# Down products of a feed-forward layer in a seven-product form, with two of four weight sums made by adding loads

## The chip, the cores and the metric

One core of a Trainium2 chip runs the whole program. The metric is the device time of one execution in microseconds, the median over runs; lower is better. The matmul engine is called PE, the vector engine DVE, the scalar engine ACT, GpSimd POOL; SP only issues DMAs.

## What is computed

One inference step of a two-layer encoder trunk for 512 prompt and 64 sample tokens, 576 columns in all, in fp32. A layer is a half-step feed-forward, three attention mixers with one output projection, a cross-attention over memory, and a second half-step feed-forward. Only the feed-forward is touched:

```
def half_ffn(x, g, w_gate, w_up, w_down):
    h = rms_norm(x, g)
    return 0.5 * ((jax.nn.silu(h @ w_gate) * (h @ w_up)) @ w_down)
```

D_MODEL is 1024 (8 row tiles of 128), D_FF is 2816 (22 tiles). There are four such blocks: two layers, two half-steps each. The sum is added to x.

## The kernel before

**Layout and precision.** Activations are transposed: a tile has 128 features as partitions and 576 tokens as columns, worked in two halves of 288 columns (`HALVES`, or L and R in the helpers). Each fp32 operand is split into a high part (a cast by ACT, at times by DVE) and a low part (what the high part leaves, a subtraction on DVE), and each product is three matmuls: high x high, high x low, low x high. Weights arrive by DMA in `stage` buffers and are split into `whi` and `wlo` (`parts`, `take`); hidden tiles into `hhi` and `hlo`.

**A feed-forward block** (`ffn`). The first 4 gate and up tiles (`PLAIN`) are ordinary products (`gemm`, banks g and u). The other 18 come in pairs through `rows2`, a seven-product form of a 2x2 block product: rows are a pair of output tiles, columns are the two halves of the tokens, and inner tiles are paired even and odd. It takes four weight blocks a11, a12, a21, a22 of 512 columns and makes four sums of them on DVE or POOL (`c1` to `c4`, tiles named `wc`); the moving side uses sums made by `combine_x`. Seven products of 4 x 3 matmuls stand in for eight. They run in PSUM banks P (a running sum that ACT copies out between products, tiles `cw`) and Q. Then `gate` applies silu, multiplies gate by up and splits the hidden tile. The down projection takes the hidden tiles in four chunks (`FFN_CHUNKS`, 4 + 6 + 6 + 6 tiles): for every chunk and each of 8 row tiles an ordinary product in bank d, after which DVE adds half of it to x (`stt` in `ffn`). Down work of a chunk is spread among the gate and up work of the next (`ffn_steps`).

**Order.** The program is first recorded as operations with costs and priorities and then put in an order by `Program.order`, a list scheduler: weight work gets an earlier priority by `ahead`, some operations may go to DVE or POOL, buffers come from pools by tag (`slots`: 49 `s` of 576 columns, 11 `b`, 3 `stage`, 6 `hi`, 6 `lo`, 8 PSUM banks). Every engine's queue is in order. All loads and stores are issued by SP.

All instructions are issued from one helper line (`issue`), so profile rows are told apart by tile names.

## Time and profile before

| | us |
|---|---|
| median of 3 runs (2452.07 to 2453.89) | 2452.24 |
| the profiled execution | 2451.2 |
| its span, first to last instruction | 2449.4 |
| PE busy | 2426.8 |
| DVE busy | 1849.4 |
| ACT busy | 1395.1 |
| POOL busy | 179.9 |

The rows further down come from that one execution. Busy time is the union of an engine's instructions; a matmul's length is its time in the pipeline, so the distance between starts tells its cost. The four feed-forward blocks lie at about 0 to 407, 840 to 1232, 1232 to 1624 and 2057 to 2449 us.

### The profile page before, as it was taken

How to read it: one execution, taken by the hardware profiler on the slowest of the kernel's cores; microseconds unless marked ns; L12 is line 12 of the kernel's file. 1: busy time of each engine (PE TensorE's matmuls, PEld its weight loads, DVE VectorE, ACT ScalarE, POOL GpSimd, SP SyncE). 2: the span in 40 equal slices, each digit the busy share in tenths (PEclk: the TensorE clock that was granted, in tenths of full speed). 3: DMA queues.
4: the chain of work that ended last, by engine and by line, in shares of the span. 5: the costliest groups of instructions: out<-in, count | busy, mean ns of one | idle time of the engine just before them, and what ended most of it. 6: DMA issues, size and time to landing. Idle time of an engine off the chain costs nothing.

```text
span 2449.4 us, 46161 instructions
## 1 busy us (share of the span) xinstructions
PE 2426.8 (99%) x18150; PEld 2387.5 (97%) x18150; DVE 1849.4 (76%) x3726; ACT 1395.1 (57%) x2857; POOL 179.9 (7%) x186
## 2 busy tenths in 40 slices
PE   8999999999999999999999999999999999999999
PEld 8999999999999999999999999999999999999999
DVE  8776766789886887776687767676898869876663
ACT  6554445679765754444455544465897666454442
POOL 1000000002110110000020000000111001100000
PEclk9999999999999999999999999999999999999999
DMA  4222333222332122223223222331223421222322
GB/s 149 93 89 84 95 102 117 67 70 87 109 132 78 53 91 89 85 87 96 91 78 96 89 93 85 108 123 56 73 87 116 130 65 66 78 93 93 93 84 91
DMA packets 77449, 224.17 MB, mean 92 GB/s; under 512 B 8880, under 2 KB 13040, under 8 KB 77232
## 3 DMA queue, kind: packets, MB, share of 16 engines
q1 hardware_dynamic: 77232, 221.23, 28.2%
q8 instruction: 142, 2.33, 0.4%
q14 instruction: 75, 0.61, 0.1%
HBM read 208.33 MB, written 12.86 MB: 90 GB/s over the span
## 4 chain that ended last, share of the span: by engine, by line
PE 89%; DVE 8%; ACT 2%; issue 1%; DMA 0%; SPq 0%; DVEq 0%; ACTq 0%
PE d L401 23%; PE P L401 19%; PE Q L401 14%; PE pj L401 7%; PE wo L401 4%; PE g L401 3%; PE u L401 3%; PE mq L401 2%; PE mo L401 2%; PE cq L401 2%; PE st L401 1%; PE O L401 1%; PE S L401 1%; PE ckv L401 1%; DVE wlo L401 1%; PE mv L401 1%
## 5 line engine op out<-in xcount | busy, mean ns | idle before, releaser
L401 ACT ACTIVATE whi<-stage 128x512 fp32r<-128x512 f32 (+1 forms) x649 | 387.8, 599 | 506.4 <-PE P L401 175.6
L401 DVE TENSOR_TENSOR wlo<-stage,whi 128x512 fp32r<-128x512 f32 (+1 forms) x706 | 466.1, 667 | 227.2 <-ACT whi L401 216.4
L401 PE MATMUL d<-hhi,wlo 128*128 128x288 f32 x1408 | 415.1, 295 | 0.0
L401 PE MATMUL d<-hlo,whi 128*128 128x288 f32 x1408 | 414.8, 295 | 0.0
L401 PE MATMUL d<-hhi,whi 128*128 128x288 f32 x1408 | 414.3, 294 | 0.0
L401 ACT ACTIVATE whi<-wc 128x512 fp32r<-128x512 f32 x280 | 177.0, 633 | 283.4 <-PE d L401 152.4
L401 DVE TENSOR_TENSOR wlo<-wc,whi 128x512 fp32r<-128x512 f32 x288 | 198.8, 690 | 145.2 <-ACT whi L401 144.1
L401 PEld LDWEIGHTS d<-hlo,whi 128*128 128x128 f32 x1408 | 264.1, 188 | 0.0
L401 PEld LDWEIGHTS d<-hhi,whi 128*128 128x128 f32 x1408 | 264.1, 188 | 0.0
L401 PEld LDWEIGHTS d<-hhi,wlo 128*128 128x128 f32 x1408 | 264.1, 188 | 0.0
L401 PE MATMUL pj<-xhi,whi 128*128 128x288 f32 x576 | 171.5, 298 | 0.0
L401 PE MATMUL P<-xbl,whi 128*128 128x288 f32 x576 | 169.8, 295 | 0.7 <-DVE xbl L401 0.7
L401 PE MATMUL P<-xbh,wlo 128*128 128x288 f32 x576 | 169.8, 295 | 0.0
L401 PE MATMUL P<-xbh,whi 128*128 128x288 f32 x576 | 169.8, 295 | 0.0
L401 PE MATMUL pj<-xhi,wlo 128*128 128x288 f32 x576 | 169.8, 295 | 0.0
L401 PE MATMUL pj<-xlo,whi 128*128 128x288 f32 x576 | 169.6, 295 | 0.0
L401 DVE SCALAR_TENSOR_TENSOR x<-d,x 128x288 f32<-128x288 f32 x256 | 113.9, 450 | 31.7 <-PE d L401 31.5
L401 DVE TENSOR_TENSOR c<-cw,Q 128x288 f32<-128x288 f32 x216 | 97.1, 450 | 26.6 <-PE Q L401 25.6
L401 PEld LDWEIGHTS pj<-xhi,whi 128*128 128x128 f32 x576 | 108.2, 188 | 1.2 <-issue 0.9
L401 PEld LDWEIGHTS P<-xbl,whi 128*128 128x128 f32 x576 | 108.3, 188 | 0.9 <-DVE xbl L401 0.9
L401 PEld LDWEIGHTS pj<-xlo,whi 128*128 128x128 f32 x576 | 108.1, 188 | 0.4
L401 PEld LDWEIGHTS P<-xbh,whi 128*128 128x128 f32 x576 | 108.3, 188 | 0.0
(433 smaller groups left out, 7401.1 us busy)
## 6 DMA issues: line engine op xcount, KB each, us to landing
stage<-wf SPq DMA_DIRECT2D x269, 512.0 KB, 3.5
stage<-wf SPq DMA_DIRECT2D x100, 384.0 KB, 3.0
stage<-wf SPq DMA_DIRECT2D x40, 256.0 KB, 2.6
o_k<-ev SPq DMA_DIRECT2D x12, 288.0 KB, 2.1
o_v<-ev SPq DMA_DIRECT2D x12, 288.0 KB, 2.5
cache<-ckv SPq DMA_DIRECT2D x12, 256.0 KB, 3.7
x<-x SPq DMA_DIRECT2D x8, 288.0 KB, 5.8
o_y<-x SPq DMA_DIRECT2D x8, 288.0 KB, 2.1
```

The source lines that it names most:

```text
L401: getattr(eng[e], fn)(**{n: real(v) for n, v in k.items()})
```

## The change

The down products are put into the seven-product form too. `wino` is now the common form for `rows2` (gate, up) and `down2` (down), after Winograd's variant: a11, a12, c2, c3, c1, c4, a22 in this order, with P and Y as running banks and Q for one product. A chunk is now two pairs of hidden tiles (the last one three), so 5 chunks, and a down step makes a pair of row tiles, 4 steps a chunk. Hidden pairs are combined by `combine_h` like the inputs. Outputs go to x partly by DVE straight from the bank, partly by a scaled copy on ACT (`dw` tiles) that DVE or POOL adds.

Of the four weight sums of a call, c3 = a11 + a21 and c1 = a22 + a21 are no longer made by an engine: the pair a11, a22 is loaded a second time, by SP, into a `wcd` buffer, and a DMA issued by POOL (`gather`, `accum_op=ALU.add`) adds a21, which stands twice in memory, to both. The sums c2 and c4 stay with DVE or POOL. c2 is c1 + a11 and c4 is c2 + a12; the minus signs sit in the sums of the moving side and in the sinks. Pools change: `stage` 2 buffers of 1536 columns, `wcd` 2 of 1024, `hi` and `lo` 8, `s` 46; rope, mask and rotary keys no longer have buffers of their own, rope and mask are loaded into `s` buffers once a layer.

```diff
-FFN_CHUNKS = ((0, 4), (4, 6), (10, 6), (16, 6))
+FFN_CHUNKS = ((0, 2), (2, 2), (4, 2), (6, 2), (8, 3))
...
+        def wino(w, m, pairs):
+            m0, m1 = _cols(2 * m * 128), _cols((2 * m + 1) * 128)
+            even, odd = [2 * p for p in pairs], [2 * p + 1 for p in pairs]
+            plan.append((w, l, None, [(k, c) for ks, c in ((odd, m0), (even, m0), (odd, m1)) for k in ks]))
+            plan.append((w, l, None, [(k, m1) for k in even + even]))
...
-    N_S = 49
+    N_S = 46
     N_B = 11
-    STAGE = 3
-    WB = 6
+    STAGE = 2
+    WC = 2
+    WB = 8
...
+    def gather(self, out, src):
+        self.p.op({"POOL": 1000.0}, [("dma_start", dict(out=out, in_=src, accum_op=ALU.add))], [out], [out],
+                  out.size() * 8 * out.shape[0] / 360.0, True)
...
         def load():
-            s2, s1 = self.fetch()[0], self.fetch()[0]
-            a21, a22, a11, a12 = s2[:, :512], s2[:, 512:], s1[:, :512], s1[:, 512:]
-            c1, c2, c3, c4 = (self.bl(F32, "wc")[:, :512] for _ in range(4))
-            self.tt(c1, a21, a22, ALU.add, self.WADD)
-            self.tt(c2, c1, a11, ALU.subtract, self.WADD)
-            self.tt(c3, a11, a21, ALU.subtract, self.WADD)
-            self.tt(c4, a12, c2, ALU.subtract, self.WADD)
+            raw, _, src = self.fetch()
+            c31 = self.new("wc", [128, 1024], F32, "wcd")[:, :2 * n]
+            self.load(c31, src[:, n:3 * n])
+            src, _, _ = self.unit_source()
+            self.gather(c31, src)
+            return raw, c31
...
+            self.tt(c2, c31[:, n:], raw[:, n:2 * n], ALU.add, self.WADD)
+            self.tt(c4, c2, raw[:, :n], ALU.add, self.WADD)
...
+        product(P, "a11", 0, True, False)
+        sinks[0](P)
...
+        Q = self.bank("Q")[:, :288]
+        product(Q, "a12", 1, True, True)
+        sinks[1](Q)
...
+        product(P, "c2", 4, False, False)
+        sinks[2](P)
...
+        Y = self.bank("Y")[:, :288]
+        product(Y, "c3", 5, True, False)
...
+        product(P, "c1", 3, False, False)
+        sinks[3](P, Y)
...
+        product(P, "c4", 2, False, True)
+        sinks[4](P)
...
+        product(Y, "a22", 6, False, True)
+        sinks[5](Y)
...
+    def down2(self, movs, xa, xb):
+        L, R = self.LR
+        w, v = self.sl(nm="dw1"), self.sl(nm="dw2")
+        E = "DVE|POOL"
+        def add(x, c):
+            return lambda ps: self.stt(x[:, c], ps, 0.5, x[:, c], ALU.mult, ALU.add)
+        def first(ps):
+            self.act(w[:, L], ps, AF.Copy, scale=0.5)
+            self.tt(xa[:, L], xa[:, L], w[:, L], ALU.add, E)
+        def third(ps, other):
+            self.act(v[:, R], ps, AF.Copy, scale=0.5)
+            add(xb, R)(other)
+            self.tt(xb, xb, v, ALU.subtract, E)
+        self.wino(movs, (first, add(xa, L), lambda ps: self.act(v[:, L], ps, AF.Copy, scale=0.5), third, add(xa, R), add(xb, L)))
...
-            hi, lo = self.sl(F32R, nm="hhi"), self.sl(F32R, nm="hlo")
-            self.split2(hi, lo, t2)
-            h[c].append((hi, lo))
...
-                for ps, cols in self.gemm("d", self.take()[0], h[c]):
-                    self.stt(x[:, cols], ps, 0.5, x[:, cols], ALU.mult, ALU.add)
+                c, m = i
+                p0, k = FFN_CHUNKS[c]
+                self.down2([movs[p] for p in range(p0, p0 + k)], self.x[2 * m], self.x[2 * m + 1])
```

Of the instructions, PE has 18,103 before and 17,575 now, DVE 3728 and 4278, ACT 2675 and 3084, POOL 191 and 505 (152 of them DMAs, where it had none), SP 541 and 575.

PE, in the first block, where down work lies between gate and up work. Before, six matmuls of the down bank d stand between two products of the running bank P:

```order
L401 MATMUL P_927<-xbh_847,whi_969 128x288
L401 MATMUL P_927<-xbl_876,whi_969 128x288
L401 MATMUL P_927<-xbh_847,wlo_986 128x288
L401 MATMUL d_1084<-hhi_357,whi_1032 128x288
L401 MATMUL d_1084<-hlo_368,whi_1032 128x288
L401 MATMUL d_1084<-hhi_357,wlo_1041 128x288
L401 MATMUL d_1084<-hhi_495,whi_1032 128x288
L401 MATMUL d_1084<-hlo_509,whi_1032 128x288
L401 MATMUL d_1084<-hhi_495,wlo_1041 128x288
L401 MATMUL P_927<-xsh_370,whi_999 128x288
L401 MATMUL P_927<-xsl_386,whi_999 128x288
L401 MATMUL P_927<-xsh_370,wlo_1005 128x288
```

Now a down call's c2 ends in its bank P, c3 runs in Y, and c1 goes on in P:

```order
L414 MATMUL P_1425<-hrh_881,whi_1429 128x288
L414 MATMUL P_1425<-hrl_887,whi_1429 128x288
L414 MATMUL P_1425<-hrh_881,wlo_1449 128x288
L414 MATMUL Y_1501<-hrh_531,whi_1358 128x288
L414 MATMUL Y_1501<-hrl_550,whi_1358 128x288
L414 MATMUL Y_1501<-hrh_531,wlo_1416 128x288
L414 MATMUL Y_1501<-hrh_881,whi_1358 128x288
L414 MATMUL Y_1501<-hrl_887,whi_1358 128x288
L414 MATMUL Y_1501<-hrh_881,wlo_1416 128x288
L414 MATMUL P_1425<-hbh_525,whi_1358 128x288
L414 MATMUL P_1425<-hbl_538,whi_1358 128x288
L414 MATMUL P_1425<-hbh_525,wlo_1416 128x288
```

Between two products of one P bank there were six matmuls of another call; now there are six of the same call, in all 37 places of this form.

POOL, in the first block. Before, sums of input tiles and weights, and then attention's work:

```order
L401 TENSOR_TENSOR wc_728<-stage_575,stage_455 128x512
L401 TENSOR_TENSOR wc_773<-stage_597 128x512
L401 TENSOR_TENSOR xt_806<-xt_806 128x288
L401 TENSOR_TENSOR wc_1987<-stage_1846 128x512
L401 TENSOR_TENSOR wc_2279<-wc_2241,stage_2236 128x512
```

Now, in the middle of the first block:

```order
L414 TENSOR_TENSOR wc_2736<-wc_2736,stage_2539 128x256
L414 TENSOR_TENSOR x0_66<-x0_66,dw1_2729 128x288
L414 DMA wcd_2758<-wf 128x1024
L414 DMA wcd_2801<-wf 128x512
L414 TENSOR_TENSOR wc_2966<-wcd_2801,stage_2811 128x256
L414 TENSOR_TENSOR wc_2966<-wc_2966,stage_2811 128x256
L414 DMA wcd_2952<-wf 128x1024
L414 TENSOR_TENSOR x2_76<-x2_76,dw1_3030 128x288
L414 DMA wcd_3000<-wf 128x512
L414 TENSOR_TENSOR ht_3101<-c1_2977,c2_3035 128x288
L414 TENSOR_TENSOR ht_3101<-ht_3101,c1_2977 128x288
L414 TENSOR_TENSOR wc_3228<-wcd_3000,stage_2990 128x256
```

POOL's queue now holds DMAs, each of which waits for the plain load of its wcd buffer, with the sums c2 (first `wc` of a pair), c4, additions to x and sums of hidden tiles between them.

DVE, in the middle of the first block. Before:

```order
L401 TENSOR_TENSOR c1_2607<-c1_2471,c1_2607 128x576
L401 TENSOR_TENSOR c2_2672<-cw1_2551,Q_2620 128x288
L401 SCALAR_TENSOR_TENSOR x3_78<-d_2656,x3_78 128x288
L401 TENSOR_TENSOR hlo_2732<-c1_2607,hhi_2719 128x576
L401 TENSOR_TENSOR c2_2672<-c2_2539,c2_2672 128x576
L401 TENSOR_TENSOR wlo_2746<-stage_2600,whi_2711 128x256
L401 TENSOR_TENSOR wc_2751<-stage_2674,stage_2635 128x512
L401 SCALAR_TENSOR_TENSOR x3_78<-d_2724,x3_78 128x288
L401 TENSOR_TENSOR hlo_2770<-c2_2672,hhi_2753 128x576
```

Now:

```order
L414 TENSOR_TENSOR wc_2904<-wcd_2758,stage_2666 128x512
L414 TENSOR_TENSOR wlo_2914<-wcd_2758,whi_2902 128x512
L414 TENSOR_TENSOR wc_2921<-wc_2904,stage_2666 128x512
L414 TENSOR_TENSOR wlo_2932<-wc_2904,whi_2919 128x512
L414 TENSOR_TENSOR wlo_2941<-wcd_2758,whi_2909 128x512
L414 TENSOR_TENSOR x1_74<-x1_74,dw2_2875 128x576
L414 TENSOR_TENSOR wlo_2960<-wc_2921,whi_2934 128x512
L414 SCALAR_TENSOR_TENSOR x0_66<-P_2708,x0_66 128x288
L414 SCALAR_TENSOR_TENSOR x1_74<-Y_2815,x1_74 128x288
L414 TENSOR_TENSOR c1_2977<-cw1_2927,Q_2923 128x288
L414 TENSOR_TENSOR wlo_2986<-wcd_2801,whi_2949 128x512
```

The sum c2 (`wc_2904`), which reads a wcd buffer, now stands at once ahead of the residuals of c3, c2, c1 and c4, and DVE's updates of x come from three banks.

## Rows read from the trace of the kernel before

**Rows 1.** The page: busy time of each engine, and two lines of its slices.
```profile
PE 2426.8 (99%) x18150; PEld 2387.5 (97%) x18150; DVE 1849.4 (76%) x3726; ACT 1395.1 (57%) x2857; POOL 179.9 (7%) x186
...
DVE  8776766789886887776687767676898869876663
...
PEclk9999999999999999999999999999999999999999
```

**Rows 2.** Busy time by stage: engine busy (instructions), clock, DMA share, GB/s.
```profile
840.40:891.30 50.90, 50.90 (x382) 50.69 (x382) 50.02 (x79) 28.53 (x47) 15.69 (x13) 1.00 0.25 84
840.40:1232.35 391.95, 391.95 (x2958) 391.74 (x2958) 287.55 (x496) 193.47 (x352) 22.29 (x18) 1.00 0.29 91
550.00:600.00 50.00, 49.19 (x351) 45.46 (x350) 48.38 (x133) 46.42 (x113) 10.51 (x14) 1.00 0.24 78
406.65:840.40 433.75, 428.33 (x3167) 409.51 (x3166) 354.81 (x863) 311.54 (x724) 47.90 (x57) 1.00 0.26 86
```

**Rows 3.** The chain of waits: its shares, and one piece (start, us, what).
```profile
PE 89%; DVE 8%; ACT 2%; issue 1%; DMA 0%; SPq 0%; DVEq 0%; ACTq 0%
...
1185.81 46.54 PE d L401 x351
```

**Rows 4.** Groups by shape, PE: the down products (busy us, mean ns | idle).
```profile
L401 PE MATMUL d<-hhi,wlo 128*128 128x288 f32 x1408 | 415.1, 295 | 0.0
L401 PE MATMUL d<-hlo,whi 128*128 128x288 f32 x1408 | 414.8, 295 | 0.0
L401 PE MATMUL d<-hhi,whi 128*128 128x288 f32 x1408 | 414.3, 294 | 0.0
```

**Rows 5.** Timeline of DVE in a block: start us, us, operation.
```profile
251.24 0.43 DVE L401 TENSOR_TENSOR wlo<-stage,whi 128x256 fp32r<-128x256 f32 x1 [0.69 <-ACT whi L401]
251.58 0.45 DVE L401 TENSOR_TENSOR c<-cw,Q 128x288 f32<-128x288 f32 x1
...
256.48 0.75 DVE L401 TENSOR_TENSOR hlo<-c,hhi 128x576 fp32r<-128x576 f32 x1
257.15 0.75 DVE L401 TENSOR_TENSOR c<-c,c 128x576 f32<-128x576 f32 x1
257.82 0.45 DVE L401 SCALAR_TENSOR_TENSOR x<-d,x 128x288 f32<-128x288 f32 x1
258.19 0.42 DVE L401 CAST whi<-wc 128x512 fp32r<-128x512 f32 x1
...
260.95 0.68 DVE L401 TENSOR_TENSOR wc<-stage,wc 128x512 f32<-128x512 f32 x1
261.55 0.45 DVE L401 SCALAR_TENSOR_TENSOR x<-d,x 128x288 f32<-128x288 f32 x1
261.92 0.68 DVE L401 TENSOR_TENSOR wc<-stage 128x512 f32<-128x512 f32 x1
```

**Rows 6.** Timeline of DVE and POOL at 1009 us.
```profile
1009.08 0.46 DVE L401 SCALAR_TENSOR_TENSOR x<-d,x 128x288 f32<-128x288 f32 x1 [0.51 <-PE d L401]
...
1009.30 1.29 POOL L401 TENSOR_TENSOR wc<-wc,stage 128x512 f32<-128x512 f32 x1 [24.37 <-DMA stage<-wf]
...
1009.45 1.42 DVE L401 TENSOR_TENSOR wlo<-stage,whi 128x256 fp32r<-128x256 f32 x1
...
1010.79 0.75 DVE L401 TENSOR_TENSOR hlo<-c,hhi 128x576 fp32r<-128x576 f32 x1
```

**Rows 7.** Groups by shape, POOL: sums of input tiles and of weights.
```profile
L401 POOL TENSOR_TENSOR xt<-xt 128x288 f32<-128x288 f32 x33 | 40.6, 1235 | 215.4 <-DVE xt L401 123.0 <-issue 91.9
L401 POOL TENSOR_TENSOR wc<-wc,stage 128x512 f32<-128x512 f32 x16 | 21.6, 1353 | 642.0 <-DMA stage<-wf 574.8 <-DVE c L401 67.2
```

**Rows 8.** Timeline of SPq (issues of SP), PE and ACT at 911 us.
```profile
911.02 0.33 SPq L401 DMA_DIRECT2D stage<-wf  x1
911.03 0.29 PE L401 MATMUL P<-xbh,wlo 128*128 128x288 f32 x1
...
911.16 0.29 PE L401 MATMUL d<-hhi,whi 128*128 128x288 f32 x1
...
911.37 0.41 ACT L401 ACTIVATE cw<-P 128x288 f32<-128x288 f32 x1 [1.10 <-PE P L401]
...
911.82 0.29 PE L401 MATMUL d<-hhi,wlo 128*128 128x288 f32 x1
...
911.96 0.29 PE L401 MATMUL P<-xsh,whi 128*128 128x288 f32 x1
```

**Rows 9.** Groups by shape, ACT: high parts of weights and of hidden tiles, copies of P.
```profile
L401 ACT ACTIVATE whi<-stage 128x512 fp32r<-128x512 f32 x551 | 346.9, 631 | 442.2 <-PE P L401 129.0 <-issue 65.4 <-PE d L401 65.3
...
L401 ACT ACTIVATE cw<-P 128x288 f32<-128x288 f32 x216 | 85.0, 394 | 8.7 <-PE P L401 8.7
...
L401 ACT ACTIVATE hhi<-c 128x576 fp32r<-128x576 f32 x72 | 49.4, 686 | 29.6 <-DVE c L401 27.5
...
L401 ACT ACTIVATE whi<-stage 128x256 fp32r<-128x256 f32 x98 | 40.9, 417 | 64.2 <-PE P L401 46.5 <-PE Q L401 13.0 <-PE d L401 4.7
```

**Rows 10.** DMA issues of weights: count, KB each, median us to landing.
```profile
stage<-wf SPq DMA_DIRECT2D x269, 512.0 KB, 3.5
```

More of the change, by code (lines that the diff above doesn't have):

```diff
@@ L59, in ffn_steps @@
             rest = rest[per:]
-        rest = [("down", c, m) for m in range(NK)]
+        rest = [("down", (c, m)) for m in range(NK // 2)]
     return steps + rest
@@ L220 @@
 class Op:
-    __slots__ = ("calls", "costs", "prio", "deps", "users", "wait", "need", "tiles", "ends", "start", "extra", "done", "port")
+    __slots__ = ("calls", "costs", "prio", "deps", "users", "wait", "need", "tiles", "ends", "start", "extra", "done", "port", "dma")
 class Program:
@@ L241, in tile, with op @@
         return t.view()
-    def op(self, costs, calls, outs, ins, extra=0.0):
+    def op(self, costs, calls, outs, ins, extra=0.0, dma=False):
         o = Op()
-        sb = sum(1 for v in ins if isinstance(v, View) and v.tile.tag != "sm" and v.size() > 1)
+        o.dma = dma
+        sb = 0 if dma else sum(1 for v in ins if isinstance(v, View) and v.tile.tag != "sm" and v.size() > 1)
         o.port = [e for e in costs if sb >= {"DVE": 2, "POOL": 1}.get(e, 99)]
@@ L569, in fetch @@
             self.p.shift -= 5.0 * c
-        return st[:, :n], u
+        return st[:, :n], u, src
     def parts(self, src):
@@ L625, in product, with split @@
+        raw, c31 = ahead(load, early=self.EARLY)
+        w = {}
+        def split(names, src):
+            hi, lo = ahead(self.parts, src)
+            for i, nm in enumerate(names):
+                w[nm] = hi[:, n * i:n * i + n], lo[:, n * i:n * i + n]
+        def product(ps, nm, i, first, last):
+            hi, lo = w[nm]
+            for k, mov in enumerate(movs):
+                xhi, xlo = mov[i]
                 o = slice(128 * k, 128 * k + 128)
-                self.mms([(ps, lhs[:, o], x, first and k == 0 and j == 0, last and k == 3 and j == 2, False)
+                self.mms([(ps, lhs[:, o], x, first and k == 0 and j == 0, last and k == len(movs) - 1 and j == 2, False)
@@ L1145, in mix @@
         attend_a(0)
+        self.rope = self.sl(nm="rope")
+        self.load(self.rope, a["rope"])
+        self.maskc = self.sl(nm="maskc")[:, :SP]
+        self.load(self.maskc, a["maskc"])
+        self.kpe = self.new("wc", [128, 1024], F32, "kpe")
+        self.memset(self.kpe[96:128], 0.0, "POOL")
         proj(1)
```

211 lines of the change are left out of this document (119 added, 92 removed).

## Prediction

> **What bounds the kernel now.** I read the page's busy line first, then the busy table by stage, then the chain of waits, then single engines. The busy line gives PE 99% of the span, DVE 76%, ACT 57%, POOL 7%, and the granted clock is 9 tenths or more in every slice, which is the 2.4 GHz level [rows 1]. In the table, the feed-forward block from 840.40 to 1232.35 us has PE busy for all of its 391.95 us [rows 2]. The chain of waits is 89% PE [rows 3]. In the feed-forward blocks the time is therefore the number of products times the rate at which PE starts them. One piece of the chain is 351 down products in 46.54 us, 132.6 ns each [rows 3]. The 295 ns that a matmul "takes" is its length in a pipeline, not its cost.
>
> **PE.** Down products now number 8 row tiles x 22 inner tiles x 2 halves x 3 = 1056 per block, 4224 in all, three groups of 1408 [rows 4]. The seven-product form keeps 7 of 8: 3696. That is 528 less, at 132.6 ns, **-70.0 us**, 17.5 us per block, so a block would last 374.5 us. Gate and up keep their count. Every microsecond of it is on the path, since PE has no idle time in a block; but it is given only while the other engines keep up.
>
> **DVE.** Its cost per instruction is the distance between starts when it runs without a gap, from the timeline: 0.67 us at 576 columns, 0.60 at 512, 0.37 at 288, 0.34 at 256 [rows 5]; I put 384 between, at 0.46. Counting both programs' instructions over four blocks:
> - weight residuals (wlo): 512 wide +64, 384 wide +112, 256 wide -32: 38.4 + 51.5 - 10.9 = +79 us;
> - weight sums left on DVE: 512 wide -134, 384 wide +26, 256 wide +32: -80.4 + 12.0 + 10.9 = -57 us. This is what the adding loads save;
> - hidden tiles: the 88 residuals hlo go (-59.0 us); 132 residuals of 576 and 44 of 288 come (+104.7), and 149 sums of 288 (+55.1): +101 us;
> - outputs: 256 updates x<-d of 288 become 320 (+23.7), and 80 subtractions of 576 and 32 additions of 288 come (+65.4): +89 us;
> - some 40 more casts and 11 sums moved from POOL: at 0.34 to 0.37, about +18 us.
>
> Together +230 us, 57 per block. DVE is busy 287.55 us in a block now [rows 2]; with 57 it is 345 of 374.5, **92%**. That is the number which decides the forecast.
>
> **DVE against POOL.** POOL loses some of the 512-wide sums and gains 256-wide sums, additions to x and sums of hidden tiles: 156 more tensor operations, 39 per block. At 1009.30 us a POOL sum runs for 1.29 us; the DVE residual that starts beside it takes 1.42 us, where 256 columns take 0.43; the x<-d just before it, whose input is in PSUM, kept its 0.46 [rows 6]. So a POOL operation can cost DVE about 1 us or nothing. Bounds per operation: 0 (the DVE operation beside it reads PSUM) to 1.2 us, the mean of POOL's 288-wide operation [rows 7]. I take 0.5, since about every fourth DVE operation in a block reads PSUM and DVE is not always at a port: 20 us per block, DVE at 365 of 374.5, 97%. The Trainium skill, in "SBUF — State Buffer", section "Who interferes with whom", has a rule against this change: a VectorE operation with two SBUF inputs and a GpSimd one that reads SBUF lock each other out for the whole instruction. The trace agrees (1.42 against 0.43 us); what it would make of the time is the second rival.
>
> What does PE lose when DVE is busy 97%? The nearest rows: from 550 to 600 us, in attention, DVE is busy 48.38 of 50 us and PE misses 0.81, 1.6%; in the block's first stage DVE is busy 50.02 of 50.90 and PE misses nothing [rows 2]. Over four blocks of 374.5 us that is 0 to 24 us. The second row is the same kind of work, weights prepared well ahead: I take **+4**.
>
> **The tile stage.** There DVE is already full [rows 2]. It gets two combinations of hidden tiles (each 3 x 0.67 + 0.37 + 4 x 0.37 = 3.9 us) and drops four residuals hlo (2.7): +5 us per block. Bounds 0 (work for later calls waits) to 5 us a block, 20 in all; the sums of the first seven-product call, 4 x 0.60 before and 2 x 0.60 now, give back a part. I take 2 a block, **+8**.
>
> **The emptying of bank P.** A down product of two pairs is 6 matmuls, 0.80 us, where a gate product has 12. In the new PE order the running sum in P is continued 37 times right after the six Y matmuls, so ACT has that long to copy P. The trace shows the same shape: the last P matmul starts at 911.03, ACT's copy runs from 911.37 for 0.41 us, and after six d matmuls P goes on at 911.96, with no wait [rows 8]. The copy ended 0.18 us before. If ACT has a 0.63 us high part in front [rows 9], PE waits up to 0.4 us. Bounds 0 to 37 x 0.4 = 15 us; ACT is busy 193.47 of 391.95 us now [rows 2] and gets about 50 more a block (240 copies of P at 0.39; high parts: 108 more of 384 columns at about 0.5, 41 more of 512 at 0.63, 45 fewer of 256 at 0.42, 37 more of 576 at 0.69 and 43 of 288 at 0.4 [rows 9]: 200 us over four blocks), 65% of the shorter block. I take half: **+7**.
>
> **The adding loads.** A call now has a wide load (stage), a plain load of the pair c3, c1 (wcd), and a load issued by POOL that adds to it. POOL waits for the plain load; behind it on POOL stand its own sums and additions. DVE's sum c2 waits for the adding load; behind it on DVE stand the residuals of c2, c3 and c1, and PE waits for those. How long an adding load of 512 KB takes no row shows. Nearest rows: a plain one lands after 3.5 us [rows 10], which is the lower end, since it moves no less; three passes (read source, read destination, write) of 3.5 make 10.5, the upper end. By the Trainium skill, "DMA: Bandwidth & Descriptors", section on the SWDGE path, such a DMA costs 2.0 us plus bytes over 436 GB/s, 3.2 us (an estimate from that page, without the adding; no run so far shows it). When does it matter? A gate or up call is 84 matmuls, 11.1 us, and a down call 42, 5.6 us; they alternate. With two wcd buffers one comes round after 16.7 us. It is held for the plain load (3.5), the adding load, one sum, and two high parts and residuals (0.60 + 2 x 0.63 + 2 x 0.69 with hops, about 3.5). So up to 16.7 - 7.0 = **9.7 us** it hides. I take 5 to 7, nearer to the plain load, and cost it at **0**. SP issues 34 more DMAs of 0.33 us each [rows 8]: nothing. The bytes of a block rise from 67,584 to 112,128 columns, 1.66 times, and the time falls to 374.5/392; the DMA share of 0.29 [rows 2] becomes 0.50, or 0.63 if adding counts double: hidden.
>
> **The end and the rest.** The last chunk of the last block has nothing after it that could fill the waits for P: **+1**. Attention keeps its instructions; 46 s buffers instead of 49 (two of them lent to rope and mask) and 2 stage buffers instead of 3 are costed at 0, covered by the deeper hi and lo pools (8 for 6); if that cover is gone, it is the third rival.
>
> **Sum** against the profiled execution (2451.2 us, span 2449.4): -70.0 + 4 + 8 + 7 + 0 + 1 = -50.0, so 2401.2. The median of the runs, 2452.24, stands 1.0 above it: **2402**.
>
> **Rivals.**
> 1. *Slower: the adding loads come late.* Beyond 9.7 us each further microsecond lengthens all of the about 72 rounds of the two wcd buffers by one, 72 us per microsecond. At the upper bound of 10.5 the time is 2382 + 58 = 2440; from 10.7 on it eats the gain, and at 12 it is 2382 + 166 = 2548. For: DVE and POOL are in order, and nothing else can go ahead of a late sum. Against: the plain load, at 3.5 us, is far below. 0.13.
> 2. *DVE becomes the bound.* If a POOL operation costs DVE 1.1 us instead of 0.5, a block needs 287.6 + 57 + 39 x 1.1 = 387.5 us of DVE, 13 more than PE's 374.5: 2382 + 52 = 2434. It decides from 0.76 us on. For: the row with 1.42 us. Against: the PSUM updates lie beside POOL's sums in the trace. 0.12.
> 3. *Fewer buffers in attention.* PE misses 5.4 of 433.75 us there [rows 2]; three times that in both layers adds 22 us to the forecast: 2424. 0.12.
>
> **Numbers.** The forecast has 0.63, with an own range of 2382 (no stall) to 2422 (two thirds of all upper bounds, 40 of 60 us). The range 2382 to 2440 takes in the third rival, most of the second, and the upper bound of the adding load. A measurement of this kernel can tell 0.2%, 5 us, from no change. Faster: the forecast, the third rival, three quarters of the second, and a little of the first, 0.86, of which I leave 0.03 for what I don't see: 0.83. Same 0.04. Slower 0.13.
>
> **What would show it.** PE instructions 528 fewer with the same distance; a block of 375 to 385 us with PE over 97% and DVE over 90%; POOL waits for wcd loads, but hardly any wait of DVE wc for a DMA. Wrong if a block shows PE idle by tens of microseconds: behind DVE wc and the DMA it is the first rival, behind DVE wlo with DVE at 100% the second. PE idle behind ACT dw by more than 15 us in total would say that P's emptying was priced too low.

## Result, and the profile after

The change made the kernel slower: 2485.38 us median (2480.78 to 2490.65) against 2452.15 us for the kernel before, measured beside it; ratio 1.0135, 95% interval 1.011 to 1.016. The forecast was 2402, with a range of 2382 to 2440. The profiled execution took 2488.79 us, span 2487.0. The page of the changed kernel (busy line, one line of slices, the chain's shares by engine and by line):

```profile
PE 2405.7 (97%) x17622; PEld 2333.4 (94%) x17622; DVE 2113.8 (85%) x4276; ACT 1549.1 (62%) x3266; POOL 487.6 (20%) x500
...
PEclk9899999999999999999999999999999999999999
...
PE 58%; DVE 25%; DMA 9%; ACT 5%; issue 2%; POOL 0%; SPq 0%; DVEq 0%; ACTq 0%; POOLq 0%
PE P L414 17%; PE Y L414 8%; DVE wlo L414 7%; PE pj L414 7%; DMA wcd<-wf 5%; PE wo L414 4%; PE Q L414 4%; DMA stage<-wf 3%; DVE c L414 3%; PE mq L414 2%; PE mo L414 2%; PE g L414 2%; DVE x L414 2%; DVE wc L414 2%; PE O L414 2%
```

Against [rows 1]: the 528 matmuls are gone, VectorE has 264 us more, GpSimd 308, of which 135 are its 152 issues of loads. Against [rows 3]: PE's share of the chain falls from 89% to 58%, and the DMAs, absent before, hold 9% of it. Where the time went shows the busy table cut at the first and the last matmul of each feed-forward stretch (block 1, attention, blocks 2 and 3, attention, block 4); the changed kernel first, the kernel before second:

```profile
6.40:420.30 413.90, 394.73 (x2848) 385.60 (x2849) 363.34 (x670) 241.55 (x473) 87.97 (x96) 0.98 0.56 152
420.30:852.50 432.20, 425.74 (x3142) 405.46 (x3141) 357.38 (x876) 307.78 (x717) 57.14 (x61) 1.00 0.29 92
852.50:1649.60 797.10, 772.55 (x5653) 756.50 (x5652) 694.00 (x1252) 466.29 (x915) 199.03 (x192) 0.99 0.54 144
1649.60:2082.70 433.10, 426.67 (x3163) 407.77 (x3162) 357.41 (x870) 310.15 (x724) 50.15 (x57) 1.00 0.29 93
2082.70:2482.70 400.00, 385.70 (x2825) 378.01 (x2824) 340.21 (x611) 220.65 (x438) 93.08 (x92) 0.99 0.52 140
```

```profile
6.60:406.40 399.80, 396.53 (x2956) 394.95 (x2957) 296.62 (x532) 203.32 (x372) 18.98 (x19) 1.00 0.32 103
406.40:840.20 433.80, 428.38 (x3166) 409.56 (x3166) 354.78 (x862) 311.41 (x725) 47.90 (x57) 1.00 0.27 86
840.20:1624.10 783.90, 783.90 (x5914) 783.48 (x5913) 572.87 (x994) 388.18 (x705) 44.22 (x36) 1.00 0.29 92
1624.10:2053.30 429.20, 425.85 (x3164) 407.78 (x3163) 349.56 (x858) 309.78 (x723) 44.87 (x52) 1.00 0.27 87
2053.30:2445.10 391.80, 391.80 (x2957) 391.59 (x2956) 274.35 (x478) 179.73 (x332) 23.75 (x18) 1.00 0.28 89
```

The feed-forward blocks together take 1611.0 us instead of 1575.5 (the sums of three rows each). With 70 us less of matmuls, TensorE loses about 105 us there that it did not lose before; some 9 of these are its clock (last section). Attention takes 865.3 instead of 863.0. VectorE is busy 694 of 797 us in blocks 2 and 3, 87%: not full. So TensorE waits many times for short spells; its weight loads name for whom, where in the kernel before each of these came to 1.1 us at most:

```profile
PEld P L414 <- ACT dw L414: 18.2, 29, 1.8
PEld Y L414 <- DVE x L414: 18.1, 26, 1.6
PEld P L414 <- ACT cw L414: 15.1, 26, 1.1
PEld P L414 <- DVE wlo L414: 9.9, 15, 1.5
```

The two engines named stand in order behind transfers. From the same waits, ScalarE's and VectorE's own. In the kernel before, ScalarE's high parts waited 13.6 us for staged tiles, and VectorE's sums 26.3 us for theirs, so the second row is no new loss in sum, but comes in fewer and longer waits (19, where there were 39):

```profile
ACT whi L414 <- DMA stage<-wf: 60.1, 56, 3.2
...
DVE wc L414 <- DMA wcd<-wf: 26.8, 19, 3.3
```

One such spell, in block 4 (timelines of GpSimd, of VectorE and of SyncE's queue, start us, us): a VectorE residual, the last reader of a target buffer (2150.04), ends at 2150.72, and SyncE at once issues the next plain load into it (2150.78). GpSimd issues the adding load behind that at 2155.54; it lands 8.1 us later, with three of SyncE's loads issued beside it, and GpSimd's sum c2 (2163.76), VectorE's c4 and all behind them wait for it.

```profile
2150.47 0.89 POOL L414 DMA_DIRECT2D wcd<-wf  x1 [6.82 <-DVE c L414]
2155.54 0.86 POOL L414 DMA_DIRECT2D wcd<-wf  x1 [4.18 <-DVE x L414]
2163.76 1.28 POOL L414 TENSOR_TENSOR wc<-wcd,stage 128x512 f32<-128x512 f32 x1 [7.37 <-DMA wcd<-wf]
2164.99 0.87 POOL L414 DMA_DIRECT2D wcd<-wf  x1
2165.60 1.10 POOL L414 TENSOR_TENSOR x<-x,dw 128x288 f32<-128x288 f32 x1
```

```profile
2150.04 0.68 DVE L414 TENSOR_TENSOR wlo<-wcd,whi 128x512 fp32r<-128x512 f32 x1
...
2162.69 0.69 DVE L414 TENSOR_TENSOR wlo<-stage,whi 128x512 fp32r<-128x512 f32 x1
2165.08 0.69 DVE L414 TENSOR_TENSOR wc<-wc,stage 128x512 f32<-128x512 f32 x1 [1.70 <-POOL wc L414]
2165.69 1.58 DVE L414 TENSOR_TENSOR wlo<-stage,whi 128x512 fp32r<-128x512 f32 x1
```

```profile
2146.05 0.33 SPq L414 DMA_DIRECT2D wcd<-wf  x1
...
2150.78 0.33 SPq L414 DMA_DIRECT2D wcd<-wf  x1
2154.91 0.33 SPq L414 DMA_DIRECT2D stage<-wf  x1
2157.57 0.33 SPq L414 DMA_DIRECT2D wcd<-wf  x1
2158.61 0.33 SPq L414 DMA_DIRECT2D stage<-wf  x1
```

The profile puts GpSimd's waits before its two issues (6.82 and 4.18 us) down to VectorE operations that neither read nor write a target buffer. What they waited for is their plain loads: those of 2146.05 and 2150.78 landed 3.7 and 4.1 us after their issue, 0.7 us before GpSimd's. The same 0.7 us is the median of all 152 adding loads of this trace, and the longest is 1.2 us.

The last rows of GpSimd and of VectorE are the second thing that matters below: the residual that starts beside GpSimd's addition takes 1.58 us where the same one took 0.69.

### The profile page after: what moved, and what is told of

Read it like the earlier page. It is cut to its first block, busy times and chain, and to the rows that moved or that the text cites. A ratio compares the mean times of both kernels' runs of the same rounds, so it can differ in the third digit from the quotient of the medians.

```text
span 2487.0 us, 46756 instructions
## 1 busy us (share of the span) xinstructions
PE 2405.7 (97%) x17622; PEld 2333.4 (94%) x17622; DVE 2113.8 (85%) x4276; ACT 1549.1 (62%) x3266; POOL 487.6 (20%) x500
## 4 chain that ended last, share of the span: by engine, by line
PE 58%; DVE 25%; DMA 9%; ACT 5%; issue 2%; POOL 0%; SPq 0%; DVEq 0%; ACTq 0%; POOLq 0%
PE P L414 17%; PE Y L414 8%; DVE wlo L414 7%; PE pj L414 7%; DMA wcd<-wf 5%; PE wo L414 4%; PE Q L414 4%; DMA stage<-wf 3%; DVE c L414 3%; PE mq L414 2%; PE mo L414 2%; PE g L414 2%; DVE x L414 2%; DVE wc L414 2%; PE O L414 2%
## 5 line engine op out<-in xcount | busy, mean ns | idle before, releaser
L414 ACT ACTIVATE whi<-stage 128x512 fp32r<-128x512 f32 (+2 forms) x565 | 335.4, 600 | 297.8 <-PE P L414 76.1
L414 DVE TENSOR_TENSOR wlo<-stage,whi 128x512 fp32r<-128x512 f32 (+2 forms) x658 | 434.4, 672 | 94.3 <-ACT whi L414 90.5
L414 POOL DMA_DIRECT2D wcd<-wf x152 | 134.9, 892 | 676.9 <-DVE wlo L414 292.6
L414 ACT ACTIVATE whi<-wc 128x512 fp32r<-128x512 f32 (+1 forms) x236 | 145.0, 614 | 110.2 <-PE P L414 53.5
L414 ACT ACTIVATE whi<-wcd 128x512 fp32r<-128x512 f32 (+1 forms) x232 | 140.6, 612 | 70.7 <-DMA wcd<-wf 23.9
L414 DVE TENSOR_TENSOR wlo<-wc,whi 128x512 fp32r<-128x512 f32 (+1 forms) x240 | 171.5, 714 | 15.2 <-ACT whi L414 14.4
L414 DVE TENSOR_TENSOR wlo<-wcd,whi 128x512 fp32r<-128x512 f32 (+1 forms) x240 | 169.2, 709 | 11.0 <-ACT whi L414 10.8
L414 ACT ACTIVATE dw<-P 128x288 f32<-128x288 f32 x240 | 96.2, 401 | 48.2 <-PE P L414 48.2
L414 PE MATMUL P<-hbh,wlo 128*128 128x288 f32 x352 | 105.6, 300 | 3.5 <-DVE wlo L414 3.5
L414 PEld LDWEIGHTS P<-xbh,wlo 128*128 128x128 f32 x576 | 108.2, 188 | 0.0
```

The lines of the kernel that those rows point to most:

```text
L414: getattr(eng[e], fn)(**{n: real(v) for n, v in k.items()})
```

## Experiments

Three theories at first. 1: the loads come late (the adding load is long, and plain loads beside it slow). 2: VectorE and GpSimd lock each other out. 3: ScalarE and VectorE empty the banks P and Y too slowly.

**The adding load, in the unchanged order.** The edit is in the call alone; the planner's table stays.

```diff
-        self.p.op({"POOL": 1000.0}, [("dma_start", dict(out=out, in_=src, accum_op=ALU.add))], [out], [out],
+        self.p.op({"POOL": 1000.0}, [("dma_start", dict(out=out[:, :16], in_=src[:, :16], accum_op=ALU.add))], [out], [out],
```

```diff
-        self.p.op({"POOL": 1000.0}, [("dma_start", dict(out=out, in_=src, accum_op=ALU.add))], [out], [out],
+        self.p.op({"POOL": 1000.0}, [("dma_start", dict(out=out, in_=src))], [out], [out],
```

> The order of the changed kernel is kept word for word; each adding load moves 16 of its columns instead of all (512, 768 or 1024), so the sums c1 and c3 hold a21 in 16 columns only: nearly all of the two sums is left out. Theory 1 (loads come late: the adding load takes 5 to 6 us, and the plain loads beside it are slowed by it): most of the loss goes, about 2405 us, 2390 to 2430, and TensorE stands idle for less than half as long. Theory 2 (VectorE and GpSimd lock each other out at their shared port, so the residuals come late): no term changes, 2480 to 2490 us. Theory 3 (banks P and Y are emptied too slowly by ScalarE and VectorE): 2480 to 2490 us as well.

> The order of the changed kernel is kept; the load that GpSimd issues writes its bytes and doesn't add them, so c3 and c1 are both a21: the two sums are left out. Tells apart two halves of theory 1. If what costs is the adding itself (a read and a write of the target for every byte), the load falls from 6.3 us for 512 KB towards the 3.6 us that a plain load on SyncE's queue takes, and the time to 2400 to 2430 us. If what costs is the issue from GpSimd behind its other work and the one more load in a chain of three, the load stays above 5 us and the time at 2455 to 2490 us. Theories 2 and 3: 2480 to 2490 us.

Measured 2452.31 (ratio 1.0003, 0.9993 to 1.0012) and 2454.92 us (1.0012, 1.0003 to 1.0022). DMA rows (KB each, median us to landing) of the change, of the plain load and of the tiny one:

```profile
wcd<-wf SPq DMA_DIRECT2D x72, 512.0 KB, 3.6
wcd<-wf POOLq DMA_DIRECT2D x72, 512.0 KB, 6.3
...
wcd<-wf POOLq DMA_DIRECT2D x64, 256.0 KB, 5.7
```

```profile
wcd<-wf POOLq DMA_DIRECT2D x72, 512.0 KB, 4.5
...
wcd<-wf POOLq DMA_DIRECT2D x64, 256.0 KB, 3.6
```

```profile
wcd<-wf POOLq DMA_DIRECT2D x152, 8.0 KB, 2.4
```

The adding lengthens a load by 1.8 and 2.1 us, and this costs 30 us. A load shorter still, by another 2.1 and 1.2 us, gives 3 us more, hardly above what can be told: the bytes of GpSimd's load are nearly free, the adding is not. (Its issue by GpSimd and a landing after 2.4 us stand in both runs, so their price is not shown.) Theory 1 holds for 30 of 83 us that separate forecast and result; 50 remain without any adding.

**Buffers, and no adding load at all.**

```diff
-    N_S = 46
+    N_S = 45
-    WC = 2
-    WB = 8
+    WC = 3
+    WB = 7
```

The second run has besides:

```diff
-                late = 900.0 if e == "SP" else 2900.0
+                late = 900.0 if e == "SP" else 4500.0
-    EARLY = 3000.0
+    EARLY = 6000.0
```

and the third, with the buffers of the change:

```diff
-            self.load(c31, src[:, n:3 * n])
             src, _, _ = self.unit_source()
-            self.gather(c31, src)
+            self.load(c31, src)
...
+            self.tt(c31, c31, raw[:, n:3 * n], ALU.add, self.WADD)
             self.tt(c2, c31[:, n:], raw[:, n:2 * n], ALU.add, self.WADD)
```

> Nothing is left out: a third buffer for the targets of the adding loads, paid for by one buffer less for the residual pairs (7 for 8) and one row-tile buffer less (45 for 46), with the order planned anew. Theory 1 in its form that there are too few buffers, so that each load starts late: 2420 to 2455 us, and SyncE's and GpSimd's waits for a freed target get shorter. If the load's own length and the shared transfer engines bind: 2475 to 2500 us. Theories 2 and 3: 2480 to 2510 us.

> The third target buffer of the earlier run (2472 us), and the planner is told that the adding load lands 1.6 us later than it was told and asks for the loads 6 us instead of 3 us of TensorE time early. Same work. If lateness of the loads is what is left of the price with three buffers: 2455 to 2468 us. If buffers, not the order, set when a load starts: 2468 to 2485 us.

> The adding load goes: SyncE loads a21 twice into the same buffer by one plain load, and one addition of up to 1024 columns on VectorE or GpSimd adds the staged a11 and a22 to it. 152 additions more, by the rows of before 1.1 us each on VectorE for 1024 columns and 0.6 us for 512, up to 130 us more of VectorE over four blocks, and 7 weight columns fetched per column pair become 5. Theory 1: the time falls to 2400 to 2440 us, since VectorE still has room. Theory 2: VectorE and GpSimd are what binds, 2500 to 2560 us, slower than the change. Theory 3: 2480 to 2490 us.

Measured 2472.31 (1.0066 to 1.0111), 2469.17 (1.0053 to 1.0083) and 2514.73 us (1.0237 to 1.027). Buffers give 13 us: in the profiled executions the feed-forward blocks get 23 us shorter, and attention, with one `s` buffer less, 9 us longer. Planned lateness on top gives 3 or nothing. The sums on the engines are worse than the adding loads by 29 us: with this planner's prices the change's reason for the loads was sound, and work on VectorE and GpSimd has a price, which theory 1 did not expect.

**The down products' own work, in the unchanged order.** The table keeps its costs; the calls touch 16 columns. The first run:

```diff
-            self.tt(xa[:, L], xa[:, L], w[:, L], ALU.add, E)
+            self.tt(xa[:, L], xa[:, L], w[:, L], ALU.add, E, 16)
-            self.tt(xb, xb, v, ALU.subtract, E)
+            self.tt(xb, xb, v, ALU.subtract, E, 16)
```

From the second run on also the three copies of P, from the third on the additions out of PSUM, in the fourth the adding load as in the first experiment:

```diff
-            self.act(w[:, L], ps, AF.Copy, scale=0.5)
+            self.act(w[:, L], ps, AF.Copy, scale=0.5, cut=16)
...
-            return lambda ps: self.stt(x[:, c], ps, 0.5, x[:, c], ALU.mult, ALU.add)
+            return lambda ps: self.stt(x[:, c], ps, 0.5, x[:, c], ALU.mult, ALU.add, 16)
```

> Order kept, adding loads kept. The two plain additions into x of each of the 80 down products (x+dw over 288 columns, x-dw over 576 columns) touch 16 columns only, so most of those sums is left out. By the rows of the changed kernel that is 60.1 us on VectorE (576 columns, 80 of them), about 13 us more there and 55.5 us on GpSimd (48 of them). Theory 2 (VectorE with GpSimd at the shared port binds): 2430 to 2455 us. Theory 1 (late loads): 2470 to 2487 us, since no load starts earlier by it. Theory 3 (banks emptied too slowly): 2470 to 2487 us.

> As the run before, and ScalarE's 240 emptyings of P for the down products copy 16 columns of 288 (401 ns each on ScalarE in the changed kernel): the halved products are left out of x but for 16 columns. Theory 3: the wait of TensorE for ScalarE's dw, 18.2 us in its weight loads, goes, and with it 20 to 35 us against the run before. Theories 1 and 2: less than 8 us against the run before, because ScalarE comes late and not because it takes long.

> As the run before, and VectorE's 240 additions out of P and Y into x (449 and 447 ns each, 107.5 us in all) touch 16 columns of 288. Nothing of what the seven products of the down part cost beside TensorE is then left but the weights' own loads, sums and residuals. Theory 2: 2400 to 2430 us. Theory 3: 2400 to 2430 us as well, most of it already in the run before. Theory 1: 2455 to 2480 us, since the loads are as late as they were.

> As the run before, and the adding loads move 16 columns each: c1 and c3 hold a21 in those alone. With the adding alone cut this small the time was 2452 us. If late loads and VectorE's load are two separate prices, they add up and this comes to the forecast, 2395 to 2410 us. If they are one price seen twice (whatever is late, the engines' queues in order pass it on), this gives at most 10 us more than the better of the two runs alone.

Measured 2462.39, 2461.26, 2451.65 and 2426.35 us (ratios 1.0040, 1.0038, 0.9996, 0.9893; each interval within 0.0017 of its ratio). The additions in SBUF cost 23 us, VectorE's additions out of PSUM 10. ScalarE's emptying cut from 288 to 16 columns gives 1 us: **theory 3 falls for ScalarE**. Its other half, VectorE's emptying, is in the 10 us: TensorE's wait of Y behind DVE x falls from 10.8 to 5.7 us with it, and whether slow emptying or VectorE's amount of work costs there, these runs don't tell. TensorE's wait behind ACT dw halves (9.9 us in the first run, 5.1 in the second) and its wait behind DVE wlo grows (10.6 to 13.7): what was late behind the copy comes next. The adding load takes off another 25 us with all this gone, of the 33 that it took off alone, so it and the additions are mostly separate prices, though not as fully as the expected 2395 to 2410 us would have it.

**Emptying by VectorE alone**, with two and with three target buffers:

```diff
-        def first(ps):
-            self.act(w[:, L], ps, AF.Copy, scale=0.5)
-            self.tt(xa[:, L], xa[:, L], w[:, L], ALU.add, E)
+        def add(x, c, f=0.5):
+            return lambda ps: self.stt(x[:, c], ps, f, x[:, c], ALU.mult, ALU.add)
...
-            self.act(v[:, R], ps, AF.Copy, scale=0.5)
+            add(xb, R, -0.5)(ps)
             add(xb, R)(other)
-            self.tt(xb, xb, v, ALU.subtract, E)
...
+        self.wino(movs, (add(xa, L), add(xa, L), add(xb, L, -0.5), third, add(xa, R), add(xb, L)))
```

> Nothing is left out. The down products' three emptyings of P through ScalarE (240 in all) and the two plain additions behind them go; VectorE adds or subtracts P into x in one instruction per place instead. Against the changed kernel that takes 96 us from ScalarE, 55 us of additions from GpSimd, and gives VectorE 240 instructions of 0.45 us for 73 us of its own: about 35 us more there. Order planned anew. If the price is GpSimd's additions at the shared port (1156 ns each for 288 columns): 2450 to 2470 us. If the price is VectorE's amount of work: 2490 to 2510 us. If only the loads count: 2480 to 2490 us.

> The third buffer for the adding loads' targets (with 7 residual pairs and 45 row tiles) and the emptying of P by VectorE alone, as in the run before. Nothing is left out. The third buffer by itself gave 2472 us. If late loads and the additions of GpSimd are two separate prices: 2440 to 2455 us. If VectorE's amount of work binds: 2475 to 2495 us.

Measured 2480.93 (1.0099 to 1.0133) and 2485.89 us (1.0113 to 1.015). Inconclusive about the additions: the planner gave GpSimd other ones in their place (page line of the first run).

```profile
PE 2401.5 (97%) x17622; PEld 2328.7 (94%) x17622; DVE 2118.8 (85%) x4363; ACT 1471.9 (59%) x3029; POOL 499.9 (20%) x490
```

77 us less on ScalarE bought 4 us, which speaks against theory 3 on ScalarE's side again.

**The prices that the planner is told.** The rows of the changed kernel show that the addition of 288 columns to x takes GpSimd 1156 ns; the planner's table says 756. (It is not short everywhere: 19 sums of hidden tiles of the same size took 821 ns.)

```profile
L414 POOL TENSOR_TENSOR x<-x,dw 128x288 f32<-128x288 f32 x48 | 55.5, 1156 | 72.3 <-ACT dw L414 72.1
```

```diff
-    return 154 + 2.09 * n
+    return 300 + 3.0 * n
```

That is the first run. The second has the other prices instead, the third all, the fourth all and the load without adding, the fifth is the kernel before with all that it has a place for, and with a small guard of the changed planner against taking two buffers where one is free:

```diff
-            costs[e] = 65 + rate * n if e == "DVE" else pool_cost(n)
+            costs[e] = 95 + rate * n if e == "DVE" else pool_cost(n)
-        c = 65 + 1.045 * in0.size() + (62 if isinstance(scalar, View) else 0)
+        c = 95 + 1.045 * in0.size() + (62 if isinstance(scalar, View) else 0)
...
-    return (51 if in_psum(src) else 94) + 0.833 * src.size() + 92 * extra
+    return (71 if in_psum(src) else 114) + 0.833 * src.size() + 92 * extra
...
-    return 66 + (1.04 if in_psum(src) else 0.52) * src.size()
+    return 96 + (1.04 if in_psum(src) else 0.52) * src.size()
...
-                late = 900.0 if e == "SP" else 2900.0
+                late = 900.0 if e == "SP" else 3500.0
```

> The same work and buffers as the changed kernel; the planner alone is told that an addition on GpSimd takes 0.30 us + 3.0 ns a column (288 columns: 1164 ns, as measured, where it was told 756). If a part of the loss is that the order takes GpSimd to be done 0.4 us before it is: 2455 to 2475 us. If the work itself or the loads are the price, whatever the order: 2480 to 2490 us.

> As the first run of this call but for GpSimd's price, which stays as the changed kernel has it (154 ns + 2.09 ns a column): VectorE, ScalarE and the adding load are told as there. If GpSimd's price was what misled the order: 2465 to 2485 us. If any of the told costs does it by itself: below 2450 us.

> Same work, same buffers as the changed kernel: the planner alone is told other costs, so the order differs. Additions on GpSimd 0.30 us + 3.0 ns a column (as in the run that gave 2460), each VectorE instruction 30 ns more (the mean pitch of additions of 288 columns standing back to back is 400 ns where it was told 366), each of ScalarE's 20 ns more, and the adding load 0.6 us later (it landed after 6.3 us for 512 KB). If the order, made with too short prices, is the price of the change: 2405 to 2440 us, faster than the kernel before. If the work binds (VectorE) or the adding load does, whatever the order: 2450 to 2470 us, no better than with GpSimd's price alone.

> The order of the run before, and GpSimd's load writes without adding (c3 and c1 are both a21: the two sums are left out). In the first order that took 30 us off. If the adding cost time only because the order expected it too early: 0 to 10 us off the run before. If the adding's length costs by itself: 20 to 35 us off.

> The kernel before, its planner told the same costs of GpSimd, VectorE and ScalarE (with the small guard of the changed planner against taking two buffers where one is free). Ordinary down products, no adding loads. If the old order was made with the same wrong prices and they didn't hurt because VectorE had room: within 6 us of 2452. If the told costs help any kernel of this kind: 2420 to 2440 us, and the gain of the run two before is not the seven-product form's.

Measured: GpSimd's price alone 2459.62 us (1.0018 to 1.004); the rest without it 2481.49 (1.0095 to 1.0132); all of them **2439.34** (0.9929 to 0.9956), faster than the kernel before with the work of the changed one; that order with a plain load 2426.19 (0.9875 to 0.990); the kernel before with the told prices 2479.43 (1.0096 to 1.0122). So much of the price was in the order, and in which engine it gives an addition to. The adding costs 13 us in the better order where it cost 30. The told prices are no general cure: they make the kernel before slower, which I did not expect and have not explained. Its blocks took 1582.8 us and attention 883.0 there, by the first and last matmuls, so attention lost most of it; the granted clock of both its stretches is 0.98 there, where it was 1.00. That the prices did this, and not the guard, is not shown.

The order that gave 2439 differs in two ways: it waits less for what is not there, and the planner, told the price, took 227 of 348 operations off GpSimd. The last two runs separate these.

**No additions on GpSimd in the feed-forward blocks** (in down2, in combine, in wino's sums and in the gating), first with the old prices, then with all the told ones.

```diff
-        E = "DVE|POOL"
+        E = "DVE"
...
-    WADD = "DVE|POOL"
+    WADD = "DVE"
```

> The changed kernel with every addition of the feed-forward blocks that could go to either engine given to VectorE; GpSimd issues the adding loads there and adds nothing. The planner's prices are those of the changed kernel, wrong ones of GpSimd's additions included, which now hardly matter. All work is done. If an addition on GpSimd costs VectorE about as much as it saves it (in the run with all prices told, 227 additions left GpSimd and VectorE's busy time fell from 2114 to 2099 us): VectorE's busy time stays within 40 us of 2114 and the kernel takes 2440 to 2465 us. If VectorE's amount of work is the bound, so that each addition moved to it is paid for: 2490 to 2510 us.

> As the run before with VectorE's, ScalarE's and the adding load's prices told as in the run that gave 2439 us, so that it differs from that run in the 100 or so additions that GpSimd kept in the feed-forward blocks. If GpSimd's additions are a loss wherever they stand: 2425 to 2437 us. If a few of them, planned with their true price, are a help: 2440 to 2450 us. In either case faster than the kernel before.

Measured 2457.02 (1.0011 to 1.0029) and **2435.87 us** (0.9931, 0.9918 to 0.9945), the fastest kernel that does all the work, though not clearly apart from the one with 2439.34 us: its GpSimd has 31 instructions less (242 for 273), not the 100 or so of the expectation. Busy lines of the two:

```profile
PE 2384.4 (97%) x17622; PEld 2326.2 (95%) x17622; DVE 2107.5 (86%) x4509; ACT 1538.8 (63%) x3249; POOL 246.8 (10%) x284
```

```profile
PE 2386.6 (98%) x17622; PEld 2334.3 (96%) x17622; DVE 2092.6 (86%) x4467; ACT 1576.5 (65%) x3333; POOL 202.2 (8%) x242
```

VectorE takes over 216 operations (233 instructions more than in the changed kernel) and is busy 6 us less. What GpSimd's additions saved VectorE they took back by lengthening what ran beside them: the residual of 512 columns wlo<-wc falls from a mean of 736 ns (first row, the changed kernel) to 689 (second row, GpSimd without additions), and x<-x,dw of 288 columns takes VectorE 456 ns where GpSimd needed 1156.

```profile
L414 DVE TENSOR_TENSOR wlo<-wc,whi 128x512 fp32r<-128x512 f32 x208 | 153.1, 736 | 10.5 <-ACT whi L414 9.8
```

```profile
L414 DVE TENSOR_TENSOR wlo<-wc,whi 128x512 fp32r<-128x512 f32 x208 | 143.0, 689 | 13.4 <-ACT whi L414 13.1
...
L414 DVE TENSOR_TENSOR x<-x,dw 128x288 f32<-128x288 f32 x80 | 36.5, 456 | 1.1 <-ACT dw L414 1.1
```

With the old prices this alone gives 28 us, as much as telling GpSimd's price (26). The page of that run has 284 instructions of GpSimd, as the run without its additions has, where the changed kernel has 500, so the price will have worked by driving additions off GpSimd. Two ways for such an addition to cost time are left: it lengthens VectorE's instructions, and its own result comes late. In the changed kernel VectorE waits 18 us and ScalarE 8 us for GpSimd's additions to x, of weights and of inputs; in the run without them neither does. No run parts the two. A third way falls: the adding loads are not held up behind GpSimd's additions, since they are issued 0.7 us after their plain load landed in both kernels (medians).

The other prices give 21 us more on top (2457 to 2436; 20 in the pair 2460 to 2439) but only 4 while GpSimd still adds (2485 to 2481). Where they give it shows the busy table of the fastest kernel, cut as before:

```profile
6.20:406.20 400.00, 387.18 (x2827) 381.46 (x2828) 355.67 (x705) 239.75 (x476) 38.01 (x47) 0.98 0.59 156
406.20:838.00 431.80, 427.65 (x3163) 409.52 (x3162) 352.91 (x874) 317.70 (x745) 32.26 (x38) 1.00 0.31 94
838.00:1624.00 786.00, 768.59 (x5685) 760.61 (x5684) 695.08 (x1356) 476.62 (x935) 65.44 (x75) 0.99 0.57 148
1624.00:2046.50 422.50, 420.53 (x3131) 403.74 (x3130) 348.13 (x867) 312.54 (x732) 35.05 (x42) 1.00 0.30 93
2046.50:2437.70 391.20, 382.44 (x2827) 378.96 (x2825) 339.42 (x665) 227.21 (x446) 31.28 (x36) 0.99 0.55 143
```

This execution took 2443.76 us, the longest of the five. Its blocks take 1577.2 us, no less than the 1575.5 of the kernel before, and its attention 854.3 instead of 863.0: what it gains lies in attention, which the told prices put in another order and the seven-product form doesn't touch. With the old prices and no additions on GpSimd the blocks take 1570.7 us (attention 870.0). So of the 70 us of matmuls, the profiled executions that do all the work show 5 at most in the blocks. The chain of the fastest kernel is close to the old one, 82% PE against 89%:

```profile
PE 82%; DVE 8%; DMA 6%; ACT 3%; issue 1%; SPq 0%; ACTq 0%; DVEq 0%; POOLq 0%
```

## Why the prediction was wrong

**Right.** TensorE's 528 matmuls are gone at an unchanged distance: twelve products of Y take 1.58 us of the chain (row below, start, us, what), 132 ns each, so they stand for -70 us. The runs that take most disturbances away, and leave sums out, come down to 2426. Attention with fewer buffers: 2.3 us more, rival 3 falls. The adding load's length: 5 to 7 us forecast, 6.3 measured.

```profile
2147.71 1.58 PE Y L414 x12
```

**Wrong: the adding load costed at 0, hidden up to 9.7 us.** The nearest statement to the truth in the text was rival 1, but with its size wrong both ways: it starts to cost between 4.5 us, where the plain load is almost free, and 6.3 us, and there it takes 30 us for some 2 us a load, not 72 a microsecond. The load's length was forecast well; what failed is the 9.7 us in which it was to hide, taken from the round of the two buffers. A plain load does start as soon as its buffer is free (0.1 us later, the median of the trace). But from the adding load's landing to the last residual out of the buffer it is 7.9 us in the median and not 3.5, for the sums, parts and residuals stand in order among other work; and 0.7 us between the plain load's landing and GpSimd's issue had no term. A round takes 18.9 us in the median instead of 16.7. Nor is the round what the adding costs: with the plain load it is 18.7, and the kernel 30 us faster. What a longer load uses up is the lead of the sums c2 and c4. Where it is gone, as in the spell above with 8.1 us beside three plain loads, they and all behind them in order start late, and the staged tile, of which only two exist now, is held as long. That this spell stands for the 30 us is argued from it, not shown. A third target buffer gave 13 us.

**Wrong: +4 for VectorE at 97%.** This step fails most. Each GpSimd operation was to cost VectorE 0.5 us; from the last runs it is 0.3 to 0.4: 233 instructions of some 0.4 us (updates of 288 columns start 0.37 us apart, [rows 5]) came to VectorE and its busy time fell by 6, so some 90 us of lengthening had gone with 216 operations; the mean lengths of the rows that both kernels have give 70. VectorE's load was even forecast too high: 57 + 20 us more a block, where blocks 2 and 3 show 60 (694.0 against 572.9 us for two). The consequence was wrong: I read what TensorE loses from a stage where weights lie ready, [rows 2], and priced an average load. The loss came at 87% busy: an operation that takes 1.58 us instead of 0.69 delays everything in order behind it, and so does a result of GpSimd that comes late; how much is each is open. Together they measure 28 us, beside rival 2's 32 above the forecast, though VectorE never became the bound. By the Trainium skill, "SBUF — State Buffer", section "Who interferes with whom", a VectorE operation with two inputs in SBUF and a GpSimd operation that reads SBUF contend for a shared pair of ports, which is an exclusive lock; the rows at 2165.60 and 2165.69 agree, 1.58 against 0.69 us, with GpSimd's addition at 1.10.

**Wrong: the order taken as good.** No term of the sum was for the planner's prices, though [rows 7] show 1235 ns for GpSimd's 288 columns and the text quoted that number. The other told prices are worth 20 us once GpSimd's additions are out, but in the profiled executions that is attention's gain, not the blocks'. What the table cost the down products would then be the additions that it put on GpSimd. That the kernel before hid a wrong table is not shown, since with the told prices it is 27 us slower.

**P's emptying, +7: the sign was misread.** The text took a wait of TensorE behind ACT dw of over 15 us as a sign that this was priced too low. The wait came, 18.2 us; but with the copy cut to 16 columns the kernel took 1 us less. The copy may be late for what stands ahead of it in ScalarE's queue, where high parts wait 60.1 us for staged tiles; no run tried that.

**The sum of it.** From 2485 the GpSimd additions take 28 us, the other prices 21 and, in that kind of order, the adding 13: 2423, if they add up. But the 21 lie in attention, so the blocks alone tell more (profiled executions): 1611.0 us as changed, 1570.7 without GpSimd's additions, 1555.3 in the told order with a plain load, which leaves two sums out; the forecast meant about 1525 (1575.5 - 50). So 56 of the 86 us have a run that takes them away, and 30 are open. Two pieces of what is left are known. At 65 us TensorE waits 5.5 us for the input combination xsh in block 1, behind the parts of a combination of hidden tiles that is new there; this was part of the tile stage's +8, and in the fastest kernel 3.4 us of it are left. It was not tried alone. The other piece is TensorE's clock, for which the sum had no term: some 16 us in the fastest kernel, 3 in the kernel before (next but one section).

## What to carry to other kernels

Price an operation given to a second engine by what it does to the first: take the length of what runs beside it, and count the helper as free only if the first engine's busy time falls. Where queues run in order, an average load says little; ask for each new wait who stands behind it and at which instant the order expects the operand. Before a planned order is judged, compare the planner's table with the measured durations: here that, with the helper's additions taken away, brought the same work from 2485 to 2436 us, as much as the whole change was expected to gain. But a truer table is no better order by itself, for the kernel before became 27 us slower with it; and a gain belongs to a change only if it lies in the stages that the change touches, so cut the time by stages before counting it.

## Unexpected of the hardware

An adding load of 512 KB lands 6.3 us after its issue, a plain one from GpSimd after 4.5, from SyncE's queue after 3.6; one of 8 KB after 2.4. By the Trainium skill, "DMA: Bandwidth & Descriptors", section "Anatomy of one DMA — SWDGE (gpsimd) path", a DMA issued there takes 2.0 us plus its bytes over 436 GB/s, 3.2 us for 512 KB (an estimate from that page); beside this kernel's other loads the measured 4.5 is more, and the adding, 1.8 more again, is not in that rule. The 8 KB load, at 2.4, is near it.

TensorE's clock: after the wait at 65 us the granted clock was 0.50, the 1.2 GHz level, from 70 to 80 us, where the kernel before had 0.84 (rows of the changed kernel, then of the one before).

```profile
60.00:70.00 10.00, 5.67 (x43) 5.40 (x41) 9.97 (x30) 3.92 (x9) 1.11 (x2) 0.88 0.16 52
70.00:80.00 10.00, 6.73 (x23) 5.66 (x24) 9.93 (x21) 4.69 (x10) 0.04 (x1) 0.50 0.53 133
```

```profile
60.00:70.00 10.00, 7.82 (x55) 7.12 (x54) 9.97 (x18) 6.05 (x11) 1.86 (x1) 0.99 0.14 52
70.00:80.00 10.00, 9.70 (x63) 9.35 (x63) 6.79 (x13) 4.29 (x10) 0.00 (x0) 0.84 0.20 54
```

Such stretches follow short idle spells of TensorE too. In the fastest kernel it was busy for 3.87 of the 6 us from 1579 us on, and then ran at 0.50:

```profile
1579.00:1585.00 6.00, 3.87 (x28) 3.40 (x26) 2.82 (x8) 1.96 (x5) 0.87 (x1) 0.98 0.81 252
1585.00:1591.50 6.50, 5.77 (x20) 4.80 (x21) 6.46 (x14) 5.46 (x12) 0.00 (x0) 0.50 0.42 62
```

Before the end of the program there are eight such stretches in the fastest kernel (44 us together), five in the changed one (38 us) and two in the kernel before (7 us). Matmuls of 288 columns mostly start 240 ns apart in them instead of 133; about 150, 112 and 31 matmuls lie there, which makes some 16, 12 and 3 us lost (estimates from these traces). So in these kernels a short wait of TensorE can cost more than its own length.
